# x loaded first in two halves, and six products of a zero tile on TensorE while x is on its way

## The chip, the cores and the metric

One core of a Trainium2 chip runs the whole program. The metric is the device time of one execution in microseconds (us). The kernel before took 1679.48 us, the median of 3 runs.

## The reference

Two transformer blocks run one after the other on one sequence of S = 256 tokens with D = 1024 features, in float32. The first step of the first block is all that the change touches:

```python
def rms_norm(x, g):
    xf = x.astype(jnp.float32)
    y = xf * lax.rsqrt(jnp.mean(xf * xf, axis=-1, keepdims=True) + EPS)
    return (y * g.astype(jnp.float32)).astype(x.dtype)

def swiglu(x, w_gu, w_down):
    gate, up = jnp.split(x @ w_gu, 2, axis=-1)
    return (jax.nn.silu(gate) * up) @ w_down
...
    h = h + 0.5 * swiglu(rms_norm(h, ffn1_norm[l]), ffn1_w_gu[l], ffn1_w_down[l])
    h = h + hybrid_mixer(rms_norm(h, mix_norm[l]), w_in[l], ...)
    h = h + 0.5 * swiglu(rms_norm(h, ffn2_norm[l]), ffn2_w_gu[l], ffn2_w_down[l])
```

A mixer (compressed, selected and window attention beside a gated recurrence), a second feed-forward part, and then a second block of two layers follow. None of their code is changed.

## The kernel before

The 256 tokens are two tiles of 128, T = 0 and T = 1, and `Net.net(T)` is one generator for each. `run` steps them in turn, T = 1 a few steps behind T = 0 (the lag starts at `LAG0` = 1 step and grows by one every `RAMP` = 8 steps, up to 3 to 6), so that each weight is used twice while it is in SBUF.

Weights come in units in the order in which they are used (`plan`). A unit is loaded by `load_unit`: each 128x512 half of it comes by one DMA on SP's queue into a tile `wr` (6 buffers, L311), then ScalarE copies it into the high part `hi` (L318) and VectorE subtracts to get the low part `lo` (L319), both into tiles `w` (42 buffers). A buffer `wr` is free when its L319 is done, and only then SP can issue the load that takes its place. Each product of a weight half is three matmuls (`mm3`, L347 to L349): hi by hi, lo weight by hi, hi weight by lo. So x needs two parts too, `xh` and `xl`.

The opening is in three places. `build` issues the first unit (`n.preload(PRE)`, two loads), then the identity matrix (128 columns of `const`, L1475), then x of tile 0 as one 128x1024 load (L1476), then the gains g1 (L1479), all on SP's queue. `first_xT` turns x: for each half of 512 columns four TensorE transposes by the identity (`tr`, L357) into a PSUM bank, ScalarE scales them by g1 into `xh` (L507), VectorE forms `xl` (L509). Then `half_stats` squares x on ScalarE (L527), and `scales` makes the row scale with a power on GpSimd (L448, L454, L493, L494). Tile 1 does the same when its x, loaded by `run` at L1429, has come. The rest of the constants (674.5 KB) is loaded by `late` at L1444, and L1460 on ScalarE waits for it.

The order on each engine is not the order of the code: a scheduler sets it at build time, by priorities and by what it expects to be ready, and the engines then run their lists strictly in that order. `high_priority(offset=HP)` moves the instructions in its block ahead of others. PSUM banks have few buffers: `mm` one for each T, `tr` one, `a` two. L580 and L584 (VectorE, in `ffn`) read a finished bank `mm`, and the next product into that bank waits for them.

Of the kernel before, what the change touches and what calls it, by code (L numbers as in the profile page):

```python
# [11 lines left out]
FT = mybir.dt.float32  # L12
FR = mybir.dt.float32r
U8 = mybir.dt.uint8
AF = mybir.ActivationFunctionType
OP = mybir.AluOpType
PSUM = bass.MemoryType.PSUM

D = 1024
S = 256  # L20
P = 128
# [8 lines left out]
AHEAD = 2  # L30
N_WR = 6
N_S2 = 20
N_W = 42
N_SE = 8
HP = 100
# [6 lines left out]
PRE = 1  # L42
# [221 lines left out]
class Net:  # L264
# [14 lines left out]
    def s2(self, cols=512, dt=FT):  # L279
        return self.t("s2", [P, cols], N_S2, dt)  # L280

    def wt(self, dt=FT):
        return self.t("w", [P, HALF], N_W, dt)

# [210 lines left out]
        return sc  # L495

    def first_xT(self, x):
        nc = self.nc
        hi, lo = self.xt_tiles()
        g = self.c["g1"]  # L500
        for j in range(2):
            pz = self.pt("mm" if j else "tr")
            for i in range(4):
                self.tr(pz[:, P * i:P * i + P], x[:, 512 * j + P * i:512 * j + P * i + P])
            parts = [(4 * j + i, pz[:, P * i:P * i + P]) for i in range(4)]
            for k, z in parts:
                nc.scalar.activation(hi[:, k, :], z, AF.Identity, scale=g[:, k:k + 1])  # L507
            for k, z in parts:
                nc.vector.scalar_tensor_tensor(lo[:, k, :], z, g[:, k:k + 1], hi[:, k, :].bitcast(FT),  # L509
                                               op0=OP.mult, op1=OP.subtract)  # L510
        st = {"v": []}
        for j in range(2):
            self.half_stats("rms", j, x, st)
        return (hi, lo), self.scales(st["v"])

    def half_stats(self, kind, j, y, st):
        nc = self.nc
# [925 lines left out]
def late(n, nc, sb, a, vec, ct):  # L1443
    nc.sync.dma_start(ct[:, P:a["const"].shape[1]], a["const"][:, P:])  # L1444
    lf = n.s2()[:, 0:64 * len(LEVELS)]
    nc.sync.dma_start(lf, a["lvl"])
    n.lvl = sb.tile([P, 64 * len(LEVELS)], U8, name="lvl")
    nc.vector.tensor_copy(n.lvl, lf)
    n.c["cpos"] = sb.tile([P, 2, 16], FT, name="cpos")
    nc.sync.dma_start(n.c["cpos"], a["cpos"])  # L1450
    n.w2 = sb.tile([P, 2, 128], FT, name="w2")
    nc.sync.dma_start(n.w2, a["w2"])
    o, w = vec["fox_b_f_2"]
    nc.sync.dma_start(n.bf, a["vec"][o:o + w].rearrange("(o w) -> o w", o=1).broadcast_to([P, w]))
    for k in ("hgrn_out_norm", "kv_norm_2", "mla_q_norm_2"):
        o, w = vec[k]
        n.small[k] = sb.tile([P, w], FT, name=k)
        nc.sync.dma_start(n.small[k], a["vec"][o:o + w].rearrange("(o w) -> o w", o=1).broadcast_to([P, w]))
    n.fsel = n.misc[:, 0:16]
    nc.scalar.activation(n.fsel, n.c["fsel"], AF.Copy)  # L1460


def build(nc, tc, a, units, offs, coff, vec):
    with tc.tile_pool(name="sb", bufs=1) as sb, tc.tile_pool(name="ps", bufs=1, space=PSUM) as ps:
        n = Net(nc, tc, sb, ps, a, units, offs)
        n.vec = vec
        xs = []
        for T in range(2):
            x = sb.tile([P, D], FT, name=f"x{T}")
            xs.append(x)  # L1470
            if T == 0:
                n.preload(PRE)
                nc0 = a["const"].shape[1]
                ct = sb.tile([P, -(-(nc0 + 24) // 32) * 32], FT, name="const")
                nc.sync.dma_start(ct[:, 0:P], a["const"][:, 0:P])  # L1475
                nc.sync.dma_start(x, a["x"][0:P, :])  # L1476
                n.c["g1"] = ct[:, nc0:nc0 + 8]
                n.bf = ct[:, nc0 + 8:nc0 + 24]
                nc.sync.dma_start(n.c["g1"], a["g1"])  # L1479
                n.x, n.small = xs, {}  # L1480
        for k, (o, w) in coff.items():
            n.c[k] = ct[:, o:o + w]
        n.misc = sb.tile([P, 32], FR, name="misc")
        n.c["mhalf"] = n.misc[:, 16:32].bitcast(FT)
        nc.gpsimd.memset(n.c["mhalf"], -0.5)
        n.late = lambda: late(n, nc, sb, a, vec, ct)
        n.run()

# [42 lines left out]
```

## Time and profile before

| | |
|---|---|
| runs | 1681.27, 1678.61, 1679.48 us (median 1679.48) |
| profiled execution | 1682.29 us |
| its span, first to last instruction | 1680.5 us |
| TensorE (PE) busy | 1649.4 us, 98% |
| VectorE (DVE) busy | 1110.6 us, 66% |
| ScalarE (ACT) busy | 936.7 us, 56% |
| DMA | 293.00 MB, mean 174 GB/s |
| mean granted clock of TensorE | 0.995 |

Busy time is a share of the span. Start times are counted from the start of the span. In a row of the timeline, the first number is the start, the second the time until the last instruction of the row ends, then come engine, line of the kernel, operation and tiles, a count, and in brackets the idle time before the row with what ended it. SPq is the queue of DMA issues of SP.

### The profile page before, as it was taken

To read this page: it belongs to the slowest core of one execution; us is meant where nothing else is said; L and a number is where in the kernel's file an instruction comes from. 1 tells how busy PE (TensorE), PEld (TensorE's weight loads), DVE (VectorE), ACT (ScalarE), POOL (GpSimd) and SP (SyncE) were. 2 spreads that over 40 slices of the span, in tenths; PEclk is the share of its full clock that TensorE was granted. 3 is DMA by queue.
4 is the path that set the end of the run, shared out by engine and by line. 5 is a ranking of instruction groups with operands and counts; after the bars stand their busy time and mean duration, and the time that the engine had idled before them with its cause. 6 is when DMAs were issued, how large, how long until landed. Compare 5 with 4: busy or idle time off the path is not lost.

```text
span 1680.5 us, 24829 instructions
## 1 busy us (share of the span) xinstructions
PE 1649.4 (98%) x8010; PEld 1345.9 (80%) x8010; DVE 1110.6 (66%) x2308; ACT 936.7 (56%) x1899; POOL 23.5 (1%) x43
## 2 busy tenths in 40 slices
PE   8999999999999999999999999999999999999997
PEld 6888777778888788877888888778888888888886
DVE  7656666666665766677558666785666865766666
ACT  7555665555555555555555555565555775555553
POOL 0000000000000000000000000000000000000000
PEclk9999999999999999999999999999999999999999
DMA  8855554336565566655436555565665633566552
GB/s 280 269 183 174 173 169 127 101 107 194 188 188 176 175 189 189 186 170 151 146 116 206 186 190 188 176 223 171 201 188 165 211 101 94 188 208 187 189 176 76
DMA packets 160403, 293.00 MB, mean 174 GB/s; under 512 B 18192, under 2 KB 27152, under 8 KB 160272
## 3 DMA queue, kind: packets, MB, share of 16 engines
q1 hardware_dynamic: 160272, 291.41, 55.7%
q8 instruction: 63, 1.03, 0.2%
q14 instruction: 68, 0.56, 0.1%
HBM read 290.29 MB, written 1.05 MB: 173 GB/s over the span
## 4 chain that ended last, share of the span: by engine, by line
PE 87%; DVE 6%; ACT 2%; DMA 2%; issue 2%; POOL 1%; SPq 0%; DVEq 0%; POOLq 0%; ACTq 0%
PE mm L347 16%; PE mm L349 15%; PE mm L348 15%; PE a L347 10%; PE a L348 10%; PE a L349 10%; PE tr L357 4%; DMA wr<-wp 1%; DVE w L319 1%; DVE x L542 1%; PE a L766 1%; ACT w L318 1%; DVE x L559 1%; DVE x L547 1%; PE a L989 1%
## 5 line engine op out<-in xcount | busy, mean ns | idle before, releaser
L319 DVE TENSOR_TENSOR w<-wr,w 128x512 fp32r<-128x512 f32 (+3 forms) x1058 | 702.8, 679 | 355.0 <-ACT w L318 171.0
L318 ACT ACTIVATE w<-wr 128x512 fp32r<-128x512 f32 (+3 forms) x1058 | 648.9, 623 | 395.1 <-PE mm L348 235.3
L347 PE MATMUL mm<-w,xh 128*128 128x512 f32 (+3 forms) x1200 | 477.5, 398 | 0.3 <-DVE s L584 0.3
L349 PE MATMUL mm<-w,xl 128*128 128x512 f32 (+3 forms) x1200 | 465.3, 388 | 0.0
L348 PE MATMUL mm<-w,xh 128*128 128x512 f32 (+3 forms) x1200 | 464.7, 387 | 0.0
L347 PEld LDWEIGHTS mm<-w,xh 128*128 128x128 f32 x1200 | 226.0, 188 | 43.9 <-issue 4.4
L349 PEld LDWEIGHTS mm<-w,xl 128*128 128x128 f32 x1200 | 225.9, 188 | 43.3
L348 PEld LDWEIGHTS mm<-w,xh 128*128 128x128 f32 x1200 | 226.6, 189 | 38.9 <-issue 0.6
L347 PE MATMUL a<-w,s 128*128 128x512 f32 x531 | 208.1, 392 | 0.5 <-ACT s L352 0.5
L348 PE MATMUL a<-w,s 128*128 128x512 f32 x531 | 207.5, 391 | 0.0
L349 PE MATMUL a<-w,s 128*128 128x512 f32 x531 | 207.3, 391 | 0.1
L347 PE MATMUL a<-w,xh 128*128 128x512 f32 (+2 forms) x304 | 119.6, 394 | 0.8 <-ACT xh L352 0.7
L347 PEld LDWEIGHTS a<-w,s 128*128 128x128 f32 x531 | 99.7, 188 | 24.9 <-issue 3.6
L348 PE MATMUL a<-w,xh 128*128 128x512 f32 (+2 forms) x304 | 118.3, 389 | 0.0
L349 PE MATMUL a<-w,xl 128*128 128x512 f32 (+2 forms) x304 | 117.2, 388 | 0.0
L349 PEld LDWEIGHTS a<-w,s 128*128 128x128 f32 x531 | 99.6, 188 | 21.1 <-DVE s L353 0.6
L348 PEld LDWEIGHTS a<-w,s 128*128 128x128 f32 x531 | 99.7, 188 | 19.9
L352 ACT ACTIVATE s<-tr 128x256 fp32r<-128x256 f32 (+2 forms) x137 | 50.6, 371 | 70.8 <-PE tr L357 70.7
L353 DVE TENSOR_TENSOR s<-tr,s 128x256 fp32r<-128x256 f32 (+2 forms) x137 | 56.4, 413 | 47.6 <-ACT s L352 47.3
L357 PE MATMUL tr<-const,s 128*128 128x128 f32 (+1 forms) x436 | 77.5, 274 | 1.9 <-DVE s L471 1.5
L357 PEld LDWEIGHTS tr<-const,s 128*128 128x128 f32 (+1 forms) x436 | 55.9, 140 | 27.6 <-DVE s L471 2.7
L347 PEld LDWEIGHTS a<-w,xh 128*128 128x128 f32 x304 | 57.4, 189 | 14.4 <-ACT xh L352 3.3
(277 smaller groups left out, 1354.9 us busy)
## 6 DMA issues: line engine op xcount, KB each, us to landing
wr<-wp SPq DMA_DIRECT2D x994, 256.0 KB, 2.7
gb<-vec SPq DMA_DIRECT2D x21, 512.0 KB, 4.3
wr<-wp SPq DMA_DIRECT2D x32, 192.0 KB, 2.4
w<-wp SPq DMA_DIRECT2D x16, 256.0 KB, 4.6
wr<-wp SPq DMA_DIRECT2D x16, 160.0 KB, 2.4
wr<-wp SPq DMA_DIRECT2D x8, 168.0 KB, 2.2
wr<-wp SPq DMA_DIRECT2D x8, 140.0 KB, 2.3
x<-x SPq DMA_DIRECT2D x2, 512.0 KB, 5.7
```

The lines of the kernel that those rows point to most:

```text
L318: nc.scalar.activation(hi[:, 0:w], r[:, 0:w], AF.Copy)
L319: nc.vector.tensor_tensor(lo[:, 0:w], r[:, 0:w], hi[:, 0:w].bitcast(FT), op=OP.subtract)
L347: mm(out, xh, wh, start=start, stop=False)
L348: mm(out, xh, wl, start=False, stop=False)
L349: mm(out, xl, wh, start=False, stop=stop)
L352: self.nc.scalar.activation(hi, src, AF.Copy)
L353: self.nc.vector.tensor_tensor(lo, src, hi.bitcast(FT), op=OP.subtract)
L357: self.nc.tensor.transpose(out, src, self.c["ident"][0:n, 0:n])
L542: nc.vector.scalar_tensor_tensor(y[:, cs], y[:, cs], nm, g[:, cs], op0=OP.add, op1=OP.mult)
L547: nc.vector.scalar_tensor_tensor(y[:, cs], y[:, cs], r, b[:, cs], op0=OP.mult, op1=OP.add)
L559: self.nc.vector.scalar_tensor_tensor(x[:, cs], acc, c, x[:, cs], op0=OP.mult, op1=OP.add, accum_out=s)
L766: nc.tensor.matmul(hp[0:2 * nb, 256 * kv:256 * kv + 256], kbs[kv][:, cc].rearrange("p g b -> p (g b)"), u[i][0], start=cc == 0, stop=cc == 15)
```

## The change

x of tile 0 comes as two loads of 512 columns, the first two on SP's queue. The identity and g1 go to ScalarE's queue. The two loads of the first weight unit follow x. `first_xT` puts the first half of the transposed x under high priority, and `first_half` holds what the loop body held. `warm` sets a tile to zero on VectorE and runs six 128x128 by 128x512 products of it on TensorE into bank `mm`; nobody reads them.

```diff
     def first_xT(self, x):
-        nc = self.nc
-        hi, lo = self.xt_tiles()
-        g = self.c["g1"]
-        for j in range(2):
...
+        xT = self.xt_tiles()
+        with self.tc.high_priority(offset=HP):
+            self.first_half(x, xT, 0)
+        self.first_half(x, xT, 1)
...
+def warm(nc, n):
+    n.T = 0
+    z = n.s2(dt=FR)
+    nc.vector.memset(z.bitcast(FT), 0.0)
+    pz = n.pt("mm")
+    for _ in range(N_WARM):
+        nc.tensor.matmul(pz, z[:, 0:P], z, start=True, stop=True)
...
-                n.preload(PRE)
                 nc0 = a["const"].shape[1]
                 ct = sb.tile([P, -(-(nc0 + 24) // 32) * 32], FT, name="const")
-                nc.sync.dma_start(ct[:, 0:P], a["const"][:, 0:P])
-                nc.sync.dma_start(x, a["x"][0:P, :])
                 n.c["g1"] = ct[:, nc0:nc0 + 8]
                 n.bf = ct[:, nc0 + 8:nc0 + 24]
-                nc.sync.dma_start(n.c["g1"], a["g1"])
+                nc.sync.dma_start(x[:, 0:512], a["x"][0:P, 0:512])
+                nc.scalar.dma_start(ct[:, 0:P], a["const"][:, 0:P])
+                nc.sync.dma_start(x[:, 512:D], a["x"][0:P, 512:D])
+                nc.scalar.dma_start(n.c["g1"], a["g1"])
+                n.preload(PRE)
...
+        warm(nc, n)
         n.late = lambda: late(n, nc, sb, a, vec, ct)
```

On TensorE, the opening stood so before (x_61 is tile 0's x and x_78 tile 1's; w_66 and w_67 are hi and lo of the first weight half, w_70 and w_71 of the second, w_126 the third):

```order
L357 MATMUL tr_9_83<-const,x_61 128x128 x4
L357 MATMUL mm_10_96<-const,x_61 128x128 x4
L347 MATMUL a_17_121<-w_66,xh_81 128x512
L348 MATMUL a_17_121<-w_67,xh_81 128x512
L349 MATMUL a_17_121<-w_66,xl_82 128x512
...
L347 MATMUL a_17_121<-w_126,xh_81 128x512
L357 MATMUL tr_32_149<-const,x_78 128x128 x4
L357 MATMUL mm_33_162<-const,x_78 128x128 x4
L348 MATMUL a_17_121<-w_127,xh_81 128x512
```

It stands so with the change (x_79 is tile 1's x, w_71 and w_72 the first weight half, w_136 the third; s_7_82 is the zero tile):

```order
L1475 MATMUL mm_8_84<-s_7_82 128x512 x5
L358 MATMUL tr_11_93<-const,x_61 128x128 x4
L1475 MATMUL mm_8_84<-s_7_82 128x512
L358 MATMUL mm_12_106<-const,x_61 128x128 x4
L348 MATMUL a_19_131<-w_71,xh_91 128x512
L349 MATMUL a_19_131<-w_72,xh_91 128x512
L350 MATMUL a_19_131<-w_71,xl_92 128x512
...
L348 MATMUL a_19_131<-w_136,xh_91 128x512
L358 MATMUL tr_34_159<-const,x_79 128x128 x4
L358 MATMUL mm_35_172<-const,x_79 128x128 x4
L349 MATMUL a_19_131<-w_137,xh_91 128x512
```

Five zero products stand ahead of the transposes of x's first half and one between the halves. The transposes of tile 1 still stand behind the seventh product of tile 0.

On VectorE, the opening before:

```order
L319 TENSOR_TENSOR w_67<-wr_62,w_66 128x512
L319 TENSOR_TENSOR w_71<-wr_64,w_70 128x512
L448 TENSOR_SCALAR col_115<-col_110,col_113 128x1
...
L509 SCALAR_TENSOR_TENSOR xl_82<-tr_9_83,const,xh_81 128x128 x4
L509 SCALAR_TENSOR_TENSOR xl_82<-mm_10_96,const,xh_81 128x128 x4
L319 TENSOR_TENSOR w_127<-wr_122,w_126 128x512
```

And with the change (wr_67 and wr_69 are the first two loaded halves, wr_132 the third):

```order
L1472 MEMSET s_7_82 128x512
L519 SCALAR_TENSOR_TENSOR xl_92<-tr_11_93,const,xh_91 128x128 x4
L320 TENSOR_TENSOR w_72<-wr_67,w_71 128x512
L519 SCALAR_TENSOR_TENSOR xl_92<-mm_12_106,const,xh_91 128x128
L320 TENSOR_TENSOR w_76<-wr_69,w_75 128x512
L519 SCALAR_TENSOR_TENSOR xl_92<-mm_12_106,const,xh_91 128x128 x3
L449 TENSOR_SCALAR col_125<-col_120,col_123 128x1
L320 TENSOR_TENSOR w_137<-wr_132,w_136 128x512
```

The splits of the first two weight halves, which stood first, now stand behind and between the parts of x.

On SP's queue, before:

```order
L311 DMA wr_62<-wp 128x512
L311 DMA wr_64<-wp 128x512
L1475 DMA const<-const 128x128
L1476 DMA x_61<-x 128x1024
L1479 DMA const<-g 128x8
...
L1429 DMA x_78<-x 128x1024
L311 DMA wr_194<-wp 128x512
L311 DMA wr_196<-wp 128x512
L1444 DMA const<-const 128x1349
L311 DMA wr_212<-wp 128x512
```

And with the change (wr_204 and wr_206 are the seventh and eighth weight half, which take the buffers of the first and second):

```order
L1491 DMA x_61<-x 128x512
L1493 DMA x_61<-x 128x512
L312 DMA wr_67<-wp 128x512
L312 DMA wr_69<-wp 128x512
...
L1435 DMA x_79<-x 128x1024
L312 DMA wr_204<-wp 128x512
L312 DMA wr_206<-wp 128x512
L1450 DMA const<-const 128x1349
L312 DMA wr_222<-wp 128x512
```

x stands ahead of the weights; the identity and g1 have left the queue. A few small loads move too: `hgrn_out_norm` (64 KB) from behind the 30th issue to the 20th, `kv_norm_2` from the 54th to the 37th. From about the 60th instruction of each engine on, the two orders are the same.

## Rows read from the trace of the kernel before

**Rows 1.** Page, part 1: busy time of each engine over the span.
```profile
PE 1649.4 (98%) x8010; PEld 1345.9 (80%) x8010; DVE 1110.6 (66%) x2308; ACT 936.7 (56%) x1899; POOL 23.5 (1%) x43
```
**Rows 2.** Waits of PE, 0 to 200 us: us in total, times, longest.
```profile
PE tr L357 <- DMA x<-x: 7.4, 1, 7.4
...
PE mm L347 <- DVE s L584: 0.3, 1, 0.3
```
**Rows 3.** Timeline of the opening, all engines and SP's queue.
```profile
0.73 1.28 ACT L318 ACT_TABLE_LOAD   x1 [0.73 <-PEq L1523]
0.74 0.86 SPq L311 DMA_DIRECT2D wr<-wp  x2
...
2.12 0.43 SPq L1476 DMA_DIRECT2D x<-x  x1
...
3.55 1.24 ACT L318 ACTIVATE w<-wr 128x512 fp32r<-128x512 f32 x2 [1.54 <-DMA wr<-wp]
...
4.97 0.53 SPq L1429 DMA_DIRECT2D x<-x  x1
5.69 1.97 SPq L311 DMA_DIRECT2D wr<-wp  x2
...
7.40 1.08 PE L357 MATMUL tr<-const,x 128*128 128x128 f32 x4 [7.40 <-DMA x<-x]
7.71 0.42 SPq L1444 DMA_DIRECT2D const<-const  x1
...
8.53 1.14 ACT L507 ACTIVATE xh<-tr,const 128x128 fp32r<-128x128 f32 x4
...
10.74 0.63 PE L347 MATMUL a<-w,xh 128*128 128x512 f32 x1
11.16 0.43 PE L348 MATMUL a<-w,xh 128*128 128x512 f32 x1
```
**Rows 4.** Timeline, 11 to 18 us.
```profile
11.58 0.68 ACT L527 ACTIVATE s<-x 128x512 f32<-128x512 f32 x1
11.90 0.60 PE L357 MATMUL tr<-const,x 128*128 128x128 f32 x4
12.70 0.48 PE L348 MATMUL a<-w,xh 128*128 128x512 f32 x1
...
16.37 0.31 ACT L1460 ACTIVATE misc<-const 128x16 fp32r<-128x16 f32 x1
16.65 0.68 DVE L319 TENSOR_TENSOR w<-wr,w 128x512 fp32r<-128x512 f32 x1
17.36 8.42 SPq L311 DMA_DIRECT2D wr<-wp  x10
```
**Rows 5.** Tile x, 0 to 30 us: its two loads, issue to landing.
```profile
DMA to landing us min/median/max: 5.1/5.7/6.3
```
**Rows 6.** Stages: us, busy of PE, PEld, DVE, ACT, POOL, PEclk, DMA share, GB/s.
```profile
2.50:3.00 0.50, 0.00 (x0) 0.00 (x0) 0.00 (x0) 0.00 (x0) 0.00 (x0) 1.00 1.05 397
6.00:6.50 0.50, 0.00 (x0) 0.00 (x0) 0.00 (x0) 0.00 (x0) 0.00 (x0) 1.00 1.00 328
18.00:18.50 0.50, 0.50 (x4) 0.40 (x3) 0.50 (x1) 0.50 (x2) 0.00 (x0) 1.00 0.14 14
```
**Rows 7.** Stages, the same columns: from 22 us to the wait of rows 2.
```profile
22.00:52.00 30.00, 29.84 (x136) 24.22 (x134) 23.81 (x44) 20.47 (x39) 0.00 (x0) 1.00 0.89 284
```
**Rows 8.** The chain that ended last, 0 to 60 us: start, us, what.
```profile
42.46 5.03 DMA wr<-wp
...
51.48 0.48 DVE s L584
```
**Rows 9.** DMA issues, 0 to 12 us: KB each, us to landing.
```profile
const<-const SPq DMA_DIRECT2D x1, 674.5 KB, 6.5
const<-const SPq DMA_DIRECT2D x1, 64.0 KB, 4.0
```
**Rows 10.** Stages with a granted clock below 1, columns as in rows 6.
```profile
339.00:345.00 6.00, 6.00 (x28) 5.78 (x27) 0.97 (x3) 0.31 (x1) 0.00 (x0) 0.50 0.00 0
...
780.00:782.00 2.00, 2.00 (x6) 1.61 (x5) 1.16 (x3) 1.22 (x7) 0.00 (x0) 0.50 0.00 0
```

More of the change, by code (lines that the diff above doesn't have):

```diff
@@ L32 @@
 N_S2 = 20
+N_WARM = 6
 N_W = 42
@@ L497, in first_xT @@
     def first_xT(self, x):
-        nc = self.nc
-        hi, lo = self.xt_tiles()
-        g = self.c["g1"]
-        for j in range(2):
[L502 to L510, printed above, removed]
+        xT = self.xt_tiles()
+        with self.tc.high_priority(offset=HP):
+            self.first_half(x, xT, 0)
+        self.first_half(x, xT, 1)
         st = {"v": []}
@@ L513, in first_xT, with first_half @@
             self.half_stats("rms", j, x, st)
-        return (hi, lo), self.scales(st["v"])
+        return xT, self.scales(st["v"])
+    def first_half(self, x, xT, j):
+        nc = self.nc
+        hi, lo = xT
+        g = self.c["g1"]
+        pz = self.pt("mm" if j else "tr")
+        for i in range(4):
+            self.tr(pz[:, P * i:P * i + P], x[:, 512 * j + P * i:512 * j + P * i + P])
+        parts = [(4 * j + i, pz[:, P * i:P * i + P]) for i in range(4)]
+        for k, z in parts:
+            nc.scalar.activation(hi[:, k, :], z, AF.Identity, scale=g[:, k:k + 1])
+        for k, z in parts:
+            nc.vector.scalar_tensor_tensor(lo[:, k, :], z, g[:, k:k + 1], hi[:, k, :].bitcast(FT),
+                                           op0=OP.mult, op1=OP.subtract)
     def half_stats(self, kind, j, y, st):
```

## The prediction

> **What bounds the kernel now.** I began with the busy times. TensorE works 1649.4 us of a span of 1680.5 us [rows 1], so some 31 us are its idle time, and only its wait at the start concerns this change. Second, I read its waits in the first 200 us [rows 2]: 7.4 us until x has landed, later 0.3 us at 52 us for bank `mm`. The reader is to see how short this list is: once TensorE has begun, it hardly waits, so what it gains at the start stays, unless a wait further on eats it. Third, I read the opening [rows 3, 4], where the change takes place. Fourth, I asked of the wait at 52 us who ended it [rows 8]: VectorE's L584, which stood behind a weight split whose load had taken 5.03 us. That wait is where the feed of weights and TensorE meet. TensorE worked 29.84 of the 30 us before it, at 0.22 us an instruction, while the DMA share was 0.89 [rows 7]. A wait that is there at all means that the feed has no slack: TensorE can pass 52 us earlier only by as much as the feed comes earlier.
>
> The end therefore moves by the smaller of two gains: P, how much earlier TensorE runs its dense stretch, and F, how much earlier the feed runs.
>
> **The change, part by part.**
>
> *x first.* Before, the first weight half was issued at 0.74 and ScalarE started on it at 3.55 us, 2.8 us later; x was issued at 2.12 and landed 5.1 us later, at 7.2 to 7.3 us [rows 3, 5]. The first half of x, with the same 256 KB, takes the weight's place: landing at 3.5 us. The identity is loaded beside it; it took 4.0 us from its issue before [rows 9], so from an issue at 0.73 us it lands at 4.7 us at the latest. Transposes thus start between 3.5 and 4.7 us; I take 3.7, since now nothing is queued ahead of it. ScalarE issues two loads (0.43 us each) before its table load of 1.28 us, and is done at 2.9 us, before x is there: nothing.
>
> *The weights behind x.* The first half is now the third load. The second load of before was split right behind the first (the row at 3.55 covers two), x's 512 KB ended at 7.3; between them I take 5.9 us for the first and 6.9 us for the second half. ScalarE: statistics (0.62 us), four `xh` (1.0 us), then at 5.9 us the first split (0.63), four `xh`, the second split at 7.5, statistics, two more splits: done at 10.0 us. VectorE: `xl` from 4.9 us, the first `lo` at 7.2, the second at 8.8, the third at 10.4 us. TensorE runs its seven first products between 6.5 and 9.7 us, where the seventh stood just ahead of the transposes of 11.90 us before [rows 4].
>
> *The zero products.* VectorE's memset costs at most the 0.68 us of a split of the same size [rows 4], at a time when VectorE had nothing to do: its first work was a `lo` behind ScalarE's split of 3.55 us [rows 3]. Products of 512 columns came 0.42 us apart in the opening, from 10.74 to 11.16 us [rows 3]; six are 2.5 us, five of them from 1.4 to 3.5 us, while x is still out, and one of 0.42 us before the second half lands. Cost: nothing, covered by x's flight; if x landed at once they would cost 2.5 us.
>
> *What is late next: x of tile 1.* In TensorE's order the transposes of tile 1 stand right behind the seventh product of tile 0, both before and now, and nothing passes them. Tile 1's x was issued at 4.97 us and landed 6.3 us later, at 11.27 [rows 3, 5]. The same bytes still stand ahead of it (two halves of x, identity, g1, six weight halves), and the DMA engines were full: share 1.05 at 2.5 us, 1.00 at 6 us [rows 6]. Its issue comes one place sooner, and I take 11.0 us; bounds 10.4 (the issue some 0.5 us sooner and all of it gained, with a little more) and 11.5 us. So TensorE, done at 9.7 us, stands still until 11.0. Before, the transposes ran from 11.90 and the next product from 12.70 us [rows 4]; now that product runs at 11.0 + 0.8 = 11.8 us. **P = 0.9 us**, bounds 0.4 and 1.5. Of the 3.7 us that x gains, most is lost here.
>
> *The feed.* ScalarE began tile 1 with its statistics at 11.58 us [rows 4] and now at 11.0: 0.6 us sooner. VectorE's order now puts each of two weight splits between parts of `xl`, and I work the row at 16.65 us (the split whose end lets SP issue the next load at 17.36 us [rows 4]) to 16.4: statistics done 15.6, the last three `xl` to 16.3, `col`, then the split. That is 0.3 us. SP now issues the seventh weight half after the first `lo` (7.2 instead of 5.69 us) and the eighth after the second (8.8 us), but the DMA engines have work until tile 1's x is in at 11.0, so the late issue opens no gap. `hgrn_out_norm`, 64 KB, leaves the busy stretch for the hole at 18 us, where the share was 0.14 [rows 6]: at 284 GB/s [rows 7] that is 0.2 us. **F = 0.5 us**, bounds 0 and 1.1.
>
> *Behind 60 us* the orders are the same, so nothing else moves but the phase of things.
>
> **The sum.** min(0.9, 0.5) = 0.5 us sooner. Against the profiled execution: 1682.29 - 0.5 = 1681.8 us. That execution stands 2.8 us above the median, so on the median's footing it is 1679.48 - 0.5 = **1679.0 us**. No change means here within 0.2%, 3.4 us, about what a measurement can tell.
>
> [...]
>
> **The rivals.**
>
> 1. *The whole head start is kept.* If tile 1's x came by 8 us, the dense stretch would start as much earlier as the first transposes: 7.4 - 3.7 = 3.7 us, 1675.8 us. For it: TensorE's longest wait is the one removed. Against it: the full DMA share and the wait at 52 us. Chance 0.07.
>
> 2. *Slower: the constants come late.* SP issued the 674.5 KB at 7.71 us, behind the eighth weight half, and they took 6.5 us [rows 3, 9], landing at 14.2. Now the eighth half waits for the second `lo` at 8.8 us, so the constants are issued at 9.3 and land at 15.8 us. ScalarE needs them in its order at 16.37 - 0.6 = 15.8 us [rows 4], ahead of weight splits on which VectorE, SP and TensorE depend. This decides from 15.8 us on: if the first weights land 1.5 us later than I took, the feed is 1.5 - 0.5 = 1.0 us behind, and the time is 1680.5 us. Chance 0.10.
>
> 3. *Slower: the clock is down when the dense stretch starts.* TensorE is half idle from 6.5 us and stands still from 9.7 to 11.0. The trace has clock drops to 0.50 behind thin stretches, at 339 and 780 us [rows 10]. [...] Chance 0.18.
>
> 4. *The drops in the middle shift.* The two of rows 10 lasted 6 and 2 us at least, and where TensorE was the bound they cost half of that, 3 and 1 us. A shift of half a us can take both away (4 us) or add another like the larger (3 us): 1675.0 to 1682.0 us. Chance 0.07. Such shifts may also be part of the 2.7 us between the runs of before.
>
> **How the numbers follow.** The forecast itself has 0.58. With bounds 0 to 1.1 us of gain and a run's spread of 1.3 us to either side, it reaches from 1677.1 to 1680.8 us; rivals 2 and 3 with part of that spread reach 1681.6. The range is 1676.4 to 1681.6 us and leaves out rival 1 and the ends of rival 4. Faster by over 0.2% is most of rival 1 and a little of rival 4: 0.07. Slower by over 0.2% needs rival 2 or 3 with an added drop: 0.03. The rest is 0.90.
>
> **What would show it.** TensorE's first transposes at 3.5 to 4.7 us; a new wait of over 1 us of its transposes for tile 1's x, ended near 11 us; the product behind them at 11.8 us; product spacing of 0.22 us from there on (else rival 3); L1466 on ScalarE not waiting for the constants (else rival 2); the wait at 52 us longer, at about 0.7 us, and ended near 51.6. A tile 1 that starts before 10 us, or a wait at 52 us that is gone, would prove me wrong.

## The result, and the profile after

The changed kernel takes **1703.72 us** (median of 4 runs, 1701.23 to 1704.14), the kernel before 1680.38 us beside it (1678.61 to 1683.52, 4 runs): ratio 1.0134, 95% interval [1.0115, 1.0153]. That is 23 us slower. The forecast was 1679.0 us, and its range ended at 1681.6.

Page of the changed kernel, part 1, answering to [rows 1]:

```profile
PE 1678.3 (99%) x8016; PEld 1351.3 (79%) x8016; DVE 1115.7 (66%) x2309; ACT 937.3 (55%) x1899; POOL 23.8 (1%) x43
```

The reader is to see that the loss is not a wait. TensorE works 28.9 us longer (1649.4 before), in a span of 1702.3 instead of 1680.5 us. Its idle time even fell, from 31.1 to 24.0 us; 28.9 - 7.1 = 21.8 us is the whole difference of the two spans.

The opening, where the change was made, looks as forecast. Timeline of TensorE, 0 to 13 us (start, duration, instruction; answers to [rows 3, 4]; PEld is TensorE's load of an operand ahead of a matmul, LDWEIGHTS):

```profile
1.45 2.50 PE L1475 MATMUL mm<-s 128*128 128x512 f32 x5 [1.45 <-DVE s L1472]
4.09 1.11 PE L358 MATMUL tr<-const,x 128*128 128x128 f32 x4
...
6.95 0.79 PE L348 MATMUL a<-w,xh 128*128 128x512 f32 x1
...
9.22 0.63 PE L348 MATMUL a<-w,xh 128*128 128x512 f32 x1
9.64 0.63 PE L349 MATMUL a<-w,xh 128*128 128x512 f32 x1
...
10.50 0.47 PE L348 MATMUL a<-w,xh 128*128 128x512 f32 x1
10.97 0.42 PEld L358 LDWEIGHTS tr<-const,x 128*128 128x128 f32 x4 [0.57 <-DMA x<-x]
10.98 0.66 PE L358 MATMUL tr<-const,x 128*128 128x128 f32 x4
...
11.83 0.48 PE L349 MATMUL a<-w,xh 128*128 128x512 f32 x1
```

x's first transposes run at 4.09 instead of 7.40 us, tile 1's at 10.98 instead of 11.90, and the product behind them at 11.83 instead of 12.70. TensorE was 0.87 us ahead of the profiled execution of before at that point; the forecast had 0.9. That lead and 23 us more were lost further on.

Where it was lost shows in the groups of one shape. Groups by line and shape, TensorE, xcount | busy us, mean ns | idle before. Products overlap, so a mean of 403 ns is longer than the step from one start to the next, 227 ns at the median before. First the kernel before:

```profile
L347 PE MATMUL mm<-w,xh 128*128 128x512 f32 x1104 | 444.5, 403 | 0.3 <-DVE s L584 0.3
L349 PE MATMUL mm<-w,xl 128*128 128x512 f32 x1104 | 434.4, 393 | 0.0
L348 PE MATMUL mm<-w,xh 128*128 128x512 f32 x1104 | 433.8, 393 | 0.0
L348 PE MATMUL a<-w,s 128*128 128x512 f32 x523 | 204.3, 391 | 0.0
...
L349 PE MATMUL mm<-w,xl 128*128 128x384 f32 x48 | 16.2, 338 | 0.0
...
L347 PE MATMUL mm<-w,keep 128*128 128x512 f32 x31 | 12.9, 415 | 0.1
```

and the changed kernel (its lines are one further down):

```profile
L348 PE MATMUL mm<-w,xh 128*128 128x512 f32 x1104 | 449.5, 407 | 0.5 <-ACT s L1089 0.5
L350 PE MATMUL mm<-w,xl 128*128 128x512 f32 x1104 | 438.8, 397 | 0.0
L349 PE MATMUL mm<-w,xh 128*128 128x512 f32 x1104 | 437.5, 396 | 0.0
...
L349 PE MATMUL a<-w,s 128*128 128x512 f32 x523 | 207.0, 396 | 0.0
...
L350 PE MATMUL mm<-w,xl 128*128 128x384 f32 x48 | 16.3, 339 | 0.0
...
L348 PE MATMUL mm<-w,keep 128*128 128x512 f32 x31 | 12.8, 414 | 0.1
```

The same instructions in the same numbers take 3 to 5 ns more each in these groups, on all three lines; the 384-column products take 1 to 3 ns more by group (this line 1 ns), and the 93 products with `keep` none (this line 1 ns less, the other two 1 ns more and 1 ns less). There are nine large groups of 128x512 products, 3 x (1104 + 523 + 272) = 5697 instructions, and their busy times add up to 25.9 us more than before, 4.5 ns each on the mean. The six zero products add 3.3 us; all the other work of TensorE together took 0.3 us less, which leaves the 28.9 us. The extra is spread over the whole kernel: a stretch without any wait holds fewer products. Stages, columns as in [rows 6], before and then changed:

```profile
420.00:504.00 84.00, 84.00 (x381) 69.20 (x380) 52.18 (x91) 45.35 (x80) 0.00 (x0) 1.00 0.60 188
924.00:1008.00 84.00, 84.00 (x382) 69.16 (x381) 52.02 (x91) 44.41 (x81) 0.00 (x0) 1.00 0.59 187
```

```profile
420.00:504.00 84.00, 84.00 (x374) 68.11 (x373) 51.09 (x88) 43.73 (x78) 0.00 (x0) 1.00 0.59 182
924.00:1008.00 84.00, 84.00 (x373) 68.08 (x372) 51.80 (x89) 43.49 (x79) 0.00 (x0) 1.00 0.59 185
```

TensorE is busy for all of the 84 us in both, at a granted clock of 1.00, with the DMA share the same; it gets 374 and 373 instructions through in place of 381 and 382. From one start to the next, consecutive 512-column products stand 227 ns apart before and 232 ns in the changed kernel (medians over more than 5000 pairs of each trace).

### The profile page after: what moved, and what is told of

It reads as the page before. It is cut to its first block, busy times and chain, and to the rows that moved or that the text cites. A ratio compares the mean times of both kernels' runs of the same rounds, so it can differ in the third digit from the quotient of the medians.

```text
span 1702.3 us, 24844 instructions
## 1 busy us (share of the span) xinstructions
PE 1678.3 (99%) x8016; PEld 1351.3 (79%) x8016; DVE 1115.7 (66%) x2309; ACT 937.3 (55%) x1899; POOL 23.8 (1%) x43
## 4 chain that ended last, share of the span: by engine, by line
PE 93%; DVE 3%; ACT 1%; issue 1%; DMA 1%; POOL 1%; POOLq 0%; DVEq 0%; ACTq 0%
PE mm L348 16%; PE mm L350 16%; PE mm L349 16%; PE a L348 11%; PE a L349 11%; PE a L350 11%; PE tr L358 5%; PE a L772 1%; PE a L1287 1%; PE a L863 1%; PE a L1266 1%; PE a L995 1%; PE a L1130 1%; DVE x L548 1%; PE mm L358 1%
## 5 line engine op out<-in xcount | busy, mean ns | idle before, releaser
L320 DVE TENSOR_TENSOR w<-wr,w 128x512 fp32r<-128x512 f32 (+3 forms) x1058 | 706.9, 680 | 362.2 <-PE mm L349 156.7
L348 PE MATMUL mm<-w,xh 128*128 128x512 f32 (+3 forms) x1200 | 482.6, 402 | 0.5 <-ACT s L1089 0.5
L349 PE MATMUL mm<-w,xh 128*128 128x512 f32 (+3 forms) x1200 | 468.5, 390 | 0.0
L348 PEld LDWEIGHTS mm<-w,xh 128*128 128x128 f32 x1200 | 227.0, 189 | 47.2 <-issue 4.4
L349 PEld LDWEIGHTS mm<-w,xh 128*128 128x128 f32 x1200 | 227.3, 189 | 41.9 <-issue 0.8
L348 PE MATMUL a<-w,s 128*128 128x512 f32 x531 | 211.0, 397 | 0.5 <-ACT s L353 0.5
L349 PE MATMUL a<-w,s 128*128 128x512 f32 x531 | 210.1, 396 | 0.0
L350 PE MATMUL a<-w,s 128*128 128x512 f32 x531 | 209.4, 395 | 0.0
L348 PE MATMUL a<-w,xh 128*128 128x512 f32 (+2 forms) x304 | 121.3, 401 | 1.0 <-ACT xh L353 0.7
L348 PEld LDWEIGHTS a<-w,s 128*128 128x128 f32 x531 | 99.9, 188 | 27.1 <-issue 4.0
L349 PE MATMUL a<-w,xh 128*128 128x512 f32 (+2 forms) x304 | 120.2, 396 | 0.5 <-DVE w L320 0.5
L349 PEld LDWEIGHTS a<-w,s 128*128 128x128 f32 x531 | 100.2, 189 | 22.0
L348 PEld LDWEIGHTS a<-w,xh 128*128 128x128 f32 x304 | 58.0, 191 | 16.2 <-ACT xh L353 3.4
```

What stands on the lines that cost most here:

```text
L320: nc.vector.tensor_tensor(lo[:, 0:w], r[:, 0:w], hi[:, 0:w].bitcast(FT), op=OP.subtract)
L348: mm(out, xh, wh, start=start, stop=False)
L349: mm(out, xh, wl, start=False, stop=False)
L350: mm(out, xl, wh, start=False, stop=stop)
```

## The experiments

**What else the diff moves.** In these programs tiles lie behind each other in SBUF in the order of their allocation, and the diff puts `n.preload(PRE)`, which allocates the weight tiles `w`, behind the allocation of `const`. Bytes per partition from the first `w` to the first of the tiles with the parts of x and the other left operands (`xh`, `xl`, `s`):

- before: 42 `w` x 2048 + `const` 6016 + `x1` 4096 + `misc` 128 = 96256 = 376 x 256. `const` has 1504 columns of 4 bytes, an odd multiple of 128.
- changed: 42 x 2048 + 4096 + 128 = 90240 = 352 x 256 + 128.

The addresses in the two built programs say the same: `xh`, `xl` and `s` begin 128 bytes behind a 256-byte boundary in both, `w` 128 bytes behind one before and on one now.

A product loads 128 columns of one of the others (PEld, 128x128, 188 to 189 ns on the mean before for the large groups) and runs 512 columns of a `w` tile (PE, 128x512). Before, both begin at the same place within 256 bytes; now they are 128 bytes apart. **Theory P** (placement): that distance makes each 512-column product 2% slower. **Rival Q**: the new order in the opening, the zero products, ScalarE's DMA queue or tile 0's PSUM banks `mm` and `tr`, which the change also swaps (`warm` takes an `mm` bank first), do it. **Rival W**: the place of the weight tiles by themselves.

**1. The change, with the old distance.** `misc`, 128 bytes, goes from behind the weight tiles to a place ahead of them; all else is the change.

```diff
+                n.misc = sb.tile([P, 32], FR, name="misc")
                 n.preload(PRE)
...
-        n.misc = sb.tile([P, 32], FR, name="misc")
```

> The changed kernel with nothing changed but where tiles lie in SBUF: the 128-byte tile misc is allocated ahead of the first weight tile, so that the weight tiles w lie 128 bytes further, at the offset to x's transposed parts that they had before the change. Theory A (the place of w against xh, xl and s sets what a 128x512 product costs): TensorE makes 192 matmuls in 42 us of dense work instead of 187, products come 227 ns apart instead of 232, and the time is 1678 to 1681 us. Theory B (the zero products, the ScalarE queue, the swapped PSUM banks or the new order cost it): the time stays at 1701 to 1704 us, products 232 ns apart.

Measured: 1680.44 us, ratio 1.0004 [0.9992, 1.0016]. Stages of this kernel, one of the two stretches above, columns as there:

```profile
420.00:504.00 84.00, 84.00 (x381) 69.21 (x380) 52.32 (x90) 45.35 (x80) 0.00 (x0) 1.00 0.60 188
```

All 23 us are gone with the zero products, the queue, the order and the banks still in place. Q falls. What is left of the change is worth nothing that can be measured.

**2. The kernel before, weight tiles moved by 128 bytes.** The same edit, made to the kernel before.

> The kernel before, same instructions in the same order; only misc is allocated ahead of the first weight tile, so that w lies 128 bytes further and xh, xl and s stay. Theory A: 230 to 232 ns a product, 1699 to 1705 us. Theory B: 1680 us, 227 ns.

Measured: 1704.66 us, ratio 1.0150 [1.0124, 1.0176]. The same stage of this kernel:

```profile
420.00:504.00 84.00, 84.00 (x373) 67.75 (x372) 50.97 (x87) 43.76 (x78) 0.00 (x0) 1.00 0.58 182
```

The whole loss, without one instruction of the change.

**3. The kernel before, the other operands moved.** `cpos`, also 128 bytes, is allocated behind the weight tiles instead of late; the weight tiles stay.

```diff
-    n.c["cpos"] = sb.tile([P, 2, 16], FT, name="cpos")
...
+                n.c["cpos"] = sb.tile([P, 2, 16], FT, name="cpos")
                 n.x, n.small = xs, {}
```

> The kernel before, same order; the 128-byte tile cpos is allocated early, behind w, so that xh, xl and s lie 128 bytes further and w stays. Theory A as a matter of the offset between the two: 230 to 232 ns and 1699 to 1705 us. Theory A as a matter of w's own address alone: 227 ns and 1680 us. Theory B: 1680 us.

Measured: 1703.26 us, ratio 1.0139 [1.0119, 1.0159]. The same stage of this kernel:

```profile
420.00:504.00 84.00, 84.00 (x372) 67.75 (x371) 51.27 (x88) 44.41 (x79) 0.00 (x0) 1.00 0.59 185
```

**4. The kernel before, both moved by 128 bytes.** The edits of 2 and 3 together.

> The kernel before, same order; both allocations moved, so that w and xh, xl, s all lie 128 bytes further and their offset is as before. Offset alone: 227 ns and 1680 us. w's own address: 230 to 232 ns and 1699 to 1705 us. Theory B: 1680 us.

Measured: 1680.48 us, ratio 1.0002 [0.9988, 1.0015]. The same stage of this kernel:

```profile
420.00:504.00 84.00, 84.00 (x382) 69.16 (x381) 52.33 (x90) 45.21 (x81) 0.00 (x0) 1.00 0.60 189
```

Runs 2, 3 and 4 settle it against W: moving either side costs 23 to 25 us (by the ratios), moving both costs nothing. It is the distance between them.

The edits move other tiles along with `w` (`wr`, `const`, x of tile 1), so another engine's traffic could still be meant. The products with `keep`, a left operand that no run moves, speak against it. `keep` begins on a 256-byte boundary before and in the changed kernel, so for these products the move of `w` takes the distance from 128 bytes to none, the other way than for all the rest. In the same execution in which the others got dearer they got cheaper: 231.7 ns from start to start before and 230.3 in the changed kernel, 229.8 in run 2 and 230.3 in run 4, and 231.6 in run 3, where neither `w` nor `keep` moves (means over 71 pairs). In run 10 below, where only the products with `keep` get another distance (192 bytes), they take 233.5 ns and those with `s` 227.2 as before. These are few products, and they win less than the others lose, but each kind goes by the distance of its own two operands.

**5 to 7. How far, and does it repeat?** Small tiles or a few columns of the constants go ahead of the weight tiles, so that these lie 64, 32 or 256 bytes further than before and the rest stays. For 64 bytes:

```diff
-    n.fsel = n.misc[:, 0:16]
...
+                n.c["mhalf"] = sb.tile([P, 16], FT, name="mhalf")
                 n.preload(PRE)
...
-        n.misc = sb.tile([P, 32], FR, name="misc")
-        n.c["mhalf"] = n.misc[:, 16:32].bitcast(FT)
+        n.fsel = sb.tile([P, 16], FR, name="fsel")
```

For 32 bytes it is `g1`, for 256 bytes 64 columns `cs` (constants `bd` to `valid`, and `g1`), whose load takes a DMA of its own:

```diff
+                cs = sb.tile([P, 64], FT, name="cs")
                 n.preload(PRE)
...
-                ct = sb.tile([P, -(-(nc0 + 24) // 32) * 32], FT, name="const")
+                ct = sb.tile([P, nc0 - 53 + 16], FT, name="const")
```

> The kernel before with the weight tiles moved by 64 bytes against the parts of x (the 64 bytes of mhalf come from misc to a place ahead of them); every instruction and its order as before. Theory A (the cost is a step: what counts is in which half of a 256-byte line the two operands begin): w now begins 192 bytes behind a 256-byte boundary, x's parts 128, the same half, so 1680 us and 381 dense products in 420 to 504 us. Theory B (the cost grows with the distance, half of it at 64 bytes): about 1692 us and some 377 products. Theory C (any unequal begin costs the whole): 1704 us and 373 products.

> The kernel before with the weight tiles moved by 32 bytes (g1's 32 bytes go from the constants to a tile ahead of them), the parts of x where they were. Theory A (step between the halves of 256 bytes): 1680 us, 381 products in 420 to 504 us. Theory B (grows with the distance): a quarter, 1686 us, 379 products. Theory C (any unequal begin costs the whole): 1704 us, 373 products.

> The kernel before with the weight tiles moved by 256 bytes (64 columns of the constants, loaded by a DMA of their own, go ahead of them), the parts of x where they were. If the cost repeats every 256 bytes: 1680 us, 381 products in 420 to 504 us. If the period is 512 bytes or more, or the cost grows on with the distance: 1704 us or more, 373 products or fewer.

Measured, 64 bytes: 1687.39 us, ratio 1.0051 [1.0034, 1.0068]. 32 bytes: 1707.54 us, 1.0174 [1.0155, 1.0193]. 256 bytes: 1679.31 us, 1.0003 [0.9994, 1.0013]. The stages of the three, in this order:

```profile
420.00:504.00 84.00, 84.00 (x378) 68.76 (x377) 52.37 (x90) 44.72 (x80) 0.00 (x0) 1.00 0.60 185
```

```profile
420.00:504.00 84.00, 84.00 (x372) 67.45 (x371) 51.19 (x88) 44.29 (x79) 0.00 (x0) 1.00 0.60 183
```

```profile
420.00:504.00 84.00, 84.00 (x382) 69.17 (x381) 52.33 (x90) 45.35 (x80) 0.00 (x0) 1.00 0.60 188
```

A distance of 256 bytes is as good as none. None of the three theories that I had written down fits the other two: 64 bytes cost a third of what 128 do (against A, which had nothing, and C, which had all; B's half was 1692), and 32 bytes cost more than 128 (against A and B).

**8. The change with the old distance, without the zero products.** Experiment 1 without the call of `warm`, so without its memset and its six products.

```diff
-        warm(nc, n)
```

> The change with the weight tiles moved by 128 bytes, as in the first experiment, and without the memset and the six zero products: only x first is left. If the zero products are worth nothing, as forecast: 1680.4 us within 2 us, x landing, the transposes of tile 1 at 11.0 us and the wait near 52 us as in the first experiment. If they held the clock up: tile 0's four transposes take 0.42 us a product's length each instead of half, the seventh product of tile 0 ends some 1 us later, but tile 1's x still sets 11.0 us, so the time still moves by less than 1 us.

Measured: 1681.01 us, ratio 1.0007 [0.9997, 1.0018], as with them. Timeline of TensorE in this kernel:

```profile
3.90 1.11 PE L358 MATMUL tr<-const,x 128*128 128x128 f32 x4 [3.90 <-DMA const<-const]
...
9.46 0.63 PE L349 MATMUL a<-w,xh 128*128 128x512 f32 x1
9.88 0.63 PE L350 MATMUL a<-w,xl 128*128 128x512 f32 x1
10.31 0.45 PE L348 MATMUL a<-w,xh 128*128 128x512 f32 x1
10.95 0.66 PE L358 MATMUL tr<-const,x 128*128 128x128 f32 x4 [0.20 <-DMA x<-x]
...
11.80 0.47 PE L349 MATMUL a<-w,xh 128*128 128x512 f32 x1
```

and in that of experiment 1, with the zero products:

```profile
8.61 0.40 PE L350 MATMUL a<-w,xl 128*128 128x512 f32 x1
8.84 0.48 PE L348 MATMUL a<-w,xh 128*128 128x512 f32 x1
...
10.32 0.63 PE L348 MATMUL a<-w,xh 128*128 128x512 f32 x1
11.04 1.11 PE L358 MATMUL tr<-const,x 128*128 128x128 f32 x4
...
12.54 0.47 PE L349 MATMUL a<-w,xh 128*128 128x512 f32 x1
```

Without them, tile 0's products stand 0.42 us apart (9.46 to 9.88). With them two stand 0.23 us apart in experiment 1 (8.61 to 8.84), close to the 227 ns of the kernel before further on, but in that execution the granted clock then fell: it is 1.00 in the stage from 7 to 8 us and 0.50 in that from 9.5 to 10.5 us, and tile 1's transposes took 1.11 in place of 0.66 us. In the changed kernel itself, which has the zero products too, tile 0's products stand 0.42 us apart (9.22 to 9.64). In all three tile 1's transposes start when its x has come and the seventh product is about done, at 10.95 to 11.04 us, and the end of experiments 1 and 8 is the same within a measurement.

**9 to 12. Other distances, and both moved by 64.** 192 and 224 bytes are made as 256 was, with 48 and 56 columns of the constants; 96 with `g1` and `mhalf`; in the tenth run `mhalf` goes ahead of the weight tiles, `cpos` behind them and `fsel` to `cpos`'s late place, which moves both sides by 64.

> The kernel before with the weight tiles moved by 192 bytes (48 columns of the constants, loaded by a DMA of their own, go ahead of them), the parts of x where they were. If the cost depends on the distance in either direction alike, with a period of 256 bytes: as at 64 bytes, 1687 us and 378 products in 420 to 504 us. If it depends on which operand begins first, the time may lie elsewhere, even below 1679 us and above 382 products: then there is a placement better than that of before.

> The kernel before with the weight tiles and the parts of x both moved by 64 bytes: their distance is that of before, but each begins 192 instead of 128 bytes behind a 256-byte boundary. If the distance alone counts: 1679.4 us within 2 us and 381 products in 420 to 504 us. If each operand's own begin counts as well: slower, toward 1687 us.

> The kernel before with the weight tiles moved by 96 bytes (g1 and mhalf as tiles of their own ahead of them), the parts of x where they were. So far 0 and 256 bytes give 1680 us, 64 give 1687, 32, 128 and 192 give 1704 to 1708. If 64 bytes are a grid, and what lies off it costs the whole: 1707 us and 372 products in 420 to 504 us, as at 32 bytes. If 32 bytes were an exception: between 64 and 128 bytes, some 1695 us and 376 products.

> The kernel before with the weight tiles moved by 224 bytes (56 columns of the constants, loaded by a DMA of their own, go ahead of them), the parts of x where they were. With a period of 256 bytes this is the weights 32 bytes ahead of the parts of x. If every distance but 0 and 64 costs the whole: 1707 us and 372 products in 420 to 504 us. If a lead in this direction is free: 1680 us or less and 381 products or more, and a placement worth keeping.

All of them in one table; products are the instructions of TensorE from 420 to 504 us:

| weight tiles moved against the others, bytes | us | ratio to before [interval] | products |
|---|---|---|---|
| 0, both moved by 64 | 1681.51 | 1.0007 [0.9992, 1.0022] | 381 |
| 0, both moved by 128 | 1680.48 | 1.0002 [0.9988, 1.0015] | 382 |
| 32 | 1707.54 | 1.0174 [1.0155, 1.0193] | 372 |
| 64 | 1687.39 | 1.0051 [1.0034, 1.0068] | 378 |
| 96 | 1707.91 | 1.0166 [1.0136, 1.0195] | 372 |
| 128 | 1704.66 | 1.0150 [1.0124, 1.0176] | 373 |
| 192 | 1707.87 | 1.0162 [1.0140, 1.0184] | 372 |
| 224 | 1705.99 | 1.0154 [1.0125, 1.0184] | 373 |
| -128 (the others moved by 128) | 1703.26 | 1.0139 [1.0119, 1.0159] | 372 |
| 256 | 1679.31 | 1.0003 [0.9994, 1.0013] | 382 |

If the cost repeats every 256 bytes, 192 bytes are 64 the other way; the two are not the same (1707.87 and 1687.39 us), so by that it matters which side lies ahead. Apart from 64, every distance tried that is not a multiple of 256 costs the whole, 1703 to 1708 us. None is better than that of before, and with it the change itself is worth nothing.

**What stays open.** The runs show that the distance decides, not which part of the chip it meets. No run shows why. Why 384-column products are spared (175 ns from start to start before, 176 in the changed kernel, medians over 158 pairs) is open too, and so is why 64 bytes cost less: there the step from L347's product to L348's has a median of 226 ns, from L348's to L349's 229 and from L349's to the next L347's 232, in the products with `xh` and `xl`.

## Why the prediction was wrong

**The step that failed** is the last term of the change: "Behind 60 us the orders are the same, so nothing else moves but the phase of things." The orders are as I read them, but an unchanged instruction did not keep its price: 5697 products got 4.5 ns dearer on the mean, 25.9 us of busy time. I followed every instruction and DMA that the diff moved, and passed over an allocation that it moved with them: the line `n.preload(PRE)` went behind `ct = sb.tile(...)`, and it allocates as well as loads. None of my rivals had a mechanism that works on all of the kernel, so the chance of slower by over 0.2% stood at 0.03, and the range ended 22 us short of the result.

Point by point, the rest:

- *x first.* Forecast for the first transposes 3.7 us, bounds 3.5 and 4.7; 4.09 with the zero products, 3.90 without, when they waited for the identity and not for x. Right within the bounds; my 3.7 went by x, but the identity, which I had dated at 4.7 at the latest, came last.
- *Tile 1's x is late next.* Forecast: landing at 11.0, next product at 11.8; the transposes ran at 10.98, the product at 11.83. Right in the times, and only half right in the reason. I had TensorE done with tile 0 at 9.7 us and a wait of over 1 us; it was done at 10.97 in the changed kernel, and the wait was 0.2 us in experiment 8. x came when TensorE was about ready: its products for tile 0 stood 0.42 us apart, and they waited for weight splits (0.45 us for L320 in the changed kernel). So by these rows an earlier x of tile 1 alone would have won little. How well 0.87 us hits 0.9 is partly luck: in experiments 2, 4 and 7, whose opening is that of before, the product that ran at 12.70 came at 12.71, 13.34 and 12.91.
- *The zero products cost nothing.* Right at the end: runs 1 and 8 agree within their intervals, with and without them. In the opening they did cost: five took 2.50 us and not 2.1, and the second half's transposes ran at 5.69 us in the changed kernel, behind the sixth, and at 4.81 without them in experiment 8. Tile 1's later start hides that.
- *The rest of the change, 0.5 us sooner.* Experiment 1 gives a ratio of 1.0004 [0.9992, 1.0016], so between 1.3 us sooner and 2.7 us slower: consistent, and too small to be told from nothing.
- *The feed and the wait at 52 us.* The chain of experiment 1, 50 to 54 us, answers to [rows 8]:

```profile
50.76 0.69 DVE w L320
...
52.04 0.48 DVE s L590
52.52 0.14 issue
52.65 0.47 PE mm L348
```

  The wait was forecast at 0.7 us and ended near 51.6. Here it took 1.0 us and ended at 52.65, so the gain was eaten there, as argued; in experiment 8 it took 0.2 us and ended at 51.17. VectorE's work that ends the wait began at 52.04 and 50.55 us, against 51.48 in [rows 8], so the feed ran 0.6 us later in one and 0.9 us earlier in the other: my bounds of 0 to 1.1 us for F were too narrow for a single execution. In the changed kernel itself the wait is gone, which I had named as proof against me. That dearer products let the feed keep up would fit experiment 2, the opening of before with dearer products: it had its product at 12.71 and no such wait. But experiments 4, 7 and 10, with cheap products and later starts (12.91 to 13.82 us), had none either, so the wait that I took for a bound on the gain comes and goes from one execution to the next.
- *Rival 2, late constants.* They were issued at 9.63 us (forecast 9.3), took 6.2 us, and L1466 on ScalarE began at 15.86 with no wait before it. It did not decide, by very little.
- *Rival 3, the clock.* It came about in experiment 1 (granted clock 0.50 from 11 to 12 us), not in the changed kernel or in experiment 8 (1.00 in both). Where it did, the product behind tile 1's transposes ran at 12.54 us, hardly ahead of 12.70, but the span of that execution, 1679.0 us, is no longer than the 1680.5 of before. My range counts a loss by this rival in its upper end, 1681.6 us; no run shows that loss, and what experiment 1 shows in its place is an end that is not later.
- *Rival 4, the drops.* Both drops of [rows 10] are in the changed kernel too, later: the stage from 360 to 370 us has a granted clock of 0.72, that from 790 to 792 us 0.50. None was added or lost, so they explain nothing of the 23 us. In experiments 1 and 8 the second is gone (granted clock 1.00 from 776 to 792 us), and the time is that of before within a measurement.
- *The clock in the opening.* Two executions with the zero products differ: in experiment 1 tile 0's products stood 0.23 us apart at 8.61, in the changed kernel 0.42 at 9.22, as without the zero products in experiment 8 (0.42 at 9.46). So it is not shown that they bring tile 0's products closer together; the stage from 9.5 to 10.5 us has a granted clock of 1.00 in the last two, with products 0.42 us apart all the same. The spacing was worth nothing at the end: tile 1's transposes, which wait for their x, began at 11.04, 10.98 and 10.95 us in the three.

## What to carry to other kernels

A diff that moves an allocation moves the address of everything behind it: read the order of the allocations as you read the order of the instructions, and compare the mean time of one unchanged instruction in a stretch without waits before you look for a new wait. In a kernel that TensorE bounds with products like these (fp32r, 128x512), try to let the tiles with the 512 columns and those with the 128 columns begin at the same place within 256 bytes per partition (227 ns a product, against 232 at a distance of 128 bytes): small tiles whose size is not a multiple of that, and the constants, go behind both or in pairs. That is shown for this kernel alone. When the span grows while TensorE's idle time falls, as here from 31.1 to 24.0 us, look for dearer instructions and not for a new wait.

## What the runs showed of the hardware that was not expected

In this kernel the time of a 128x512 product depends on where its two operands lie in SBUF to each other: 227 ns from start to start where their begins differ by a multiple of 256 bytes, 232 ns at 128 bytes. The cost is 24 to 28 us of 1680, or 1.4 to 1.7%, at 32, 96, 128, 192 and 224 bytes, and 8 us at 64 bytes. Products of 384 columns took 1 to 3 ns more at 128 bytes in the changed kernel. Moving both operands together, by 64 or 128 bytes, changes nothing that can be measured (1681.51 and 1680.48 us).
